# A hybrid encoder trunk on one core: one full tile traded for a value tile and a half tile, and other load costs in the planner

## The chip, the core and the metric

The kernel runs on one core of a Trainium2 chip. The core has a matrix engine (TensorE, called PE here; PEld is its loading of weights, which overlaps the matmuls), a vector engine (DVE), a scalar engine (ACT), GpSimd (POOL) and a sync engine (SP), which here issues every DMA. Each engine works through its own queue in order. Operands lie in SBUF, matmul results in banks of PSUM, and the inputs, the outputs and some intermediate tensors in DRAM.

The metric is the device time of one execution in microseconds. A version is timed in several runs, and their median counts.

## The reference

Two sequences (prompt and sample, each of 1024 positions of width 1024, float32) go through the same trunk of two layers. Each layer computes one projection into twelve blocks of 256 columns, four mixers, a gate for each, an output projection and a residual:

```python
def mixer_layer(x, norm_g, w_in, w_out, ...):
    hdn = rmsnorm(x, norm_g)
    z = jnp.einsum('bsd,dp->bsp', hdn, w_in)
    (a_v, a_g, b_q, b_k, b_v, b_g, c_u, c_g, d_q, d_k, d_v, d_g) = jnp.split(z, N_BLOCKS, axis=-1)
    y_a = pool_mixer(a_v, pool_w, pool_scale) * jax.nn.silu(a_g)
    y_b = dilated_attention(rope(heads(b_q)), rope(heads(b_k)), heads(b_v)).reshape(bsz, s, GROUP_W)
    y_b = y_b * jax.nn.silu(b_g)
    y_c = s5_mixer(c_u, a_re, a_im, log_dt, b_re, b_im, c_re, c_im, ssm_d, glu_w, glu_b) * jax.nn.silu(c_g)
    y_d = neighbourhood_attention(heads(d_q), heads(d_k), heads(d_v), na_rpb).reshape(bsz, s, GROUP_W)
    y_d = y_d * jax.nn.silu(d_g)
    y = jnp.concatenate([y_a, y_b, y_c, y_d], axis=-1)
    return x + jnp.einsum('bsm,md->bsd', y, w_out)

def trunk(x):
    for l in range(DEPTH):                 # DEPTH = 2
        x = mixer_layer(x, norm_g[l], w_in[l], w_out[l], ...)
    return rmsnorm(x, final_g)
```

The mixers are pooling over windows of 2 to 16 positions, attention in three dilated windows with rotary embedding, a bidirectional diagonal state space model (S5) and attention in a two-dimensional neighbourhood of 8 by 16 positions of a 16 by 64 grid. The heads are 64 wide, four in each attention.

## The kernel before

**Four passes.** The layers run in the order prompt, sample in layer 0, and then prompt, sample in layer 1; I number these passes 0 to 3. The x of a pass stays in SBUF, column major, as a high and a low part (`xh`, `xl`, eight tiles of 128 by 1024 each), so that a float32 product is made of three matmuls: `vz<-xh,whi`, `vz<-xl,whi` and `vz<-xh,wlo`. The parts of the weights, `whi` and `wlo`, are made from a loaded tile `raw` by ACT and POOL and kept in DRAM for the sample. These projections are most of PE's work.

**Steps.** A pass is made of steps, each a *thread* of operations, listed in `STEPS`: `setup0`/`setup1` (tables of the S5 mixer for a layer: POOL makes products `E` of tables named `turns`, which go to DRAM as `Rd`), `na` (neighbourhood attention), `sq` (sum of squares of the sample's x, function `sum_squares`), `poolw0`/`poolw1` (function `pool_weights`: the matrix `w_av` times `pool_w`, matmuls `rb<-th,wavt`, which makes the weights `wav` of the pooling mixer), `dil` (dilated attention, which ends with `combine`), `ssm` and `sout` (S5, in quads of groups that load `UM`, `Cm`, `R` and `B` and work on `X` and `H` on DVE), `pool`, `x` (normalisation of the next x), and the out stages (`out6723`, `out`), which load the old x into a tile `p`, add, and store.

**Neighbourhood attention.** For each of four heads `h` and four column windows `w`, sixteen windows in a pass, the loop in `neighbourhood` loads four pieces of 64 KB of values from `vd` in DRAM into a tile `nv` (group `v`) and, for some windows, a bias; it then makes scores, a softmax and transposes, splits the result into a tile `D`, and multiplies with the values in `outer` (six matmuls `no<-D,nv`, the last readers of `nv`).

**The list schedule.** No instruction is issued where it is written. Every call goes to a `Recorder`, which keeps the operations with what they depend on (`record`). `order` then plans: it walks through time with a cost for each operation (`cost`), a latency between engines (`LAT`), and a model of DMA, and each time an engine is free, it takes the ready operation of lowest `prio` for which there are buffers. Whether there are is the answer of `room`, which reserves for every earlier thread the most that it will still want of a group. Then `emit` replays the operations in the planned order, so that all instructions bear one line in the trace, L467 (L469 after the change). The plan decides which instruction stands before which on each queue and which tile goes into which buffer; when they run is decided on the chip by semaphores.

**Buffers.** SBUF is divided into groups of tiles of one size, counted in `SIZES`: `A`, full tiles of 128 partitions by 4 KB; `z`, *half tiles* of 128 by 2 KB; `v`, value tiles `nv` of 128 by 2 KB; `p`, tiles of the old x; `raw`, `whi`, `wlo`, `D` and others. A trace names a buffer after the first tile that lay in it: the six half tiles appear as `wto`, `th`, `fold` and `zq`, whatever they hold, and PSUM banks as `vz`, `kt`, `ss`, `rb` and `no`. So the weights `pool_w` land in a tile called `th`, and a load of the sample's x for `sq` reads `wto<-in_x`.

Of the kernel before, what the change touches and what calls it, by code (L numbers as in the profile page):

```python
# [145 lines left out]
def overlap(a, b):  # L146
    return a[0] <= b[1] and b[0] <= a[1] and (a[2] is None or b[2] is None or a[2] & b[2])


class Op:  # L150
    __slots__ = ("eng", "method", "args", "kw", "reads", "writes", "idx", "prio", "thread", "cost", "deps", "outs", "n", "ready", "end", "tiles", "pos", "start", "s", "e", "ev")


class Thread:
# [22 lines left out]
class Recorder:  # L177
# [61 lines left out]

    def record(self, eng, method, args, kw):  # L240
        op = Op()
        reserve, after = kw.pop("reserve", ()), kw.pop("after", None)
        op.eng, op.method, op.args, op.kw = NAMES[eng], method, args, kw
        pos = [a for a in args if isinstance(a, View)]
        op.writes = [kw[k] for k in ("out", "accum_out") if k in kw]
        if "out" not in kw:
            op.writes.insert(0, pos.pop(0))
        op.reads = pos + [v for k, v in kw.items() if isinstance(v, View) and k not in ("out", "accum_out")]
        op.idx, op.thread = len(self.ops), self.thread
        op.prio = op.idx + self.cls + self.base  # L250
        op.cost = self.cost(op)
        op.tiles = []
        deps = {}
        for write, views in ((False, op.reads), (True, op.writes)):
            for v in views:
                t = v.tile
                if t.space == "IO":
                    continue
                if t not in op.tiles:
                    op.tiles.append(t)  # L260
                whole = t.space == "PSUM"
                r = (0, 127, None) if whole else v.region()
                keep = []
                for o, w, q in t.accesses:
                    hit = (w or write) and overlap(q, r)
                    if hit and o is not op:
                        raw = w and not write
                        deps[o] = deps.get(o, False) or raw or o.eng != op.eng

                    covered = hit and write and o is not op and (whole or (r[2] is not None and r[0] <= q[0] and q[1] <= r[1] and q[2] | r[2] == r[2]))  # L270
                    if not covered:
                        keep.append((o, w, q))
                keep.append((op, write, r))
                t.accesses = keep
        if after is None and not deps:
            after = self.thread.ops[-1] if self.thread.ops else self.gate
        if after:
            deps.setdefault(after, False)
        op.deps = deps
        for v in reserve:  # L280
            if v.tile not in op.tiles:
                op.tiles.append(v.tile)
        for t in op.tiles:
            if not t.users:
                t.thread = self.thread
            t.users.append(op)
            t.left += 1
        op.pos = len(op.thread.ops)
        op.thread.ops.append(op)
        self.ops.append(op)  # L290
        return op
# [18 lines left out]
    def order(self):  # L310
# [14 lines left out]
        dma = 0.0  # L325
        done, result, now = 0, [], 0.0
# [42 lines left out]
        while done < len(self.ops):  # L369
            progress = False  # L370
            for e in engines:
# [3 lines left out]
                while q and q[0][0] <= now:  # L375
                    _, _, op = heapq.heappop(q)
                    heapq.heappush(r, (op.prio, op.idx, op))
                aside, pick, full = [], None, {}
                while r:
                    x = heapq.heappop(r)  # L380
# [8 lines left out]
                op, progress = pick, True  # L389
# [11 lines left out]
                if e == "SP":  # L401
                    v = op.writes[0]
                    size = 4
                    for _, n in v.dims:
                        size *= n
                    dma = max(dma, now + 1100) + size / 360.0
                    op.end = dma + 900
                result.append(op)
                done += 1
                th = op.thread  # L410
# [15 lines left out]
                for o, raw in op.outs:  # L426
                    lat = LAT.get((e, o.eng), 130)
                    if o.eng != e and o.thread.patient:
                        lat += SLACK
                    when = op.end + lat if raw else now  # L430
                    o.ready = max(o.ready, when)
                    o.n -= 1
                    if o.n == 0:
                        heapq.heappush(later[o.eng], (max(o.ready, now), o.idx, o))
# [9 lines left out]
            now = min(times)  # L444
# [32 lines left out]
    return v.rearrange("p (c j) -> p c j", c=4)  # L477


SIZES = dict(A=21, raw=2, whi=3, wlo=3, z=6, p=3, D=2, rs=2, v=1)  # L480
LATE, SOON = 10**6, -(10**6)
XLEAD, YLEAD, OB, RES, XG, NAORD, DILORD, NAHOLD, DILHOLD, NALOOP = 2, 3, ('mm', 's'), 1, 'p', ((('v', 'q'), ('q',)), (('v', 'q'), ('q',))), (('q', 'v'), ('q',)), -1, 0, 0
VB, FOLD = ('mm', 'mm', 'mm', 's'), 'vector'
# [5 lines left out]
class Kernel:  # L489
    def __init__(self, rec, T, nseq, depth, dbg=None):  # L490
        self.nc, self.nseq, self.depth = rec, nseq, depth
        self.T = {n: rec.extern(n, ap) for n, ap in T.items()}
        self.dbg = None if dbg is None else rec.extern("dbg", dbg)
        for name, n in SIZES.items():
            rec.group(name, n)
# [677 lines left out]
    def pool_weights(self, l):  # L1173

        nc = self.nc
        for m in range(2):
            made = self.own([128, 8, 128], "wav", F32, "DRAM")
            wt, pw = self.slot([128, S], "wavt"), self.z("pool_w")[:, :128]
            nc.sync.dma_start(out=wt, in_=self.T["w_av"][l, m])
            nc.sync.dma_start(out=pw, in_=self.T["pool_w"][:, l, m])  # L1180
            for i in range(2):
                ps, t = self.bank("t", "wav"), self.z("wav")
                for k in range(4):
                    nc.tensor.matmul(ps[:, 128 * k : 128 * k + 128], wt[:, 512 * i + 128 * k : 512 * i + 128 * k + 128], pw, start=True, stop=True)
                nc.scalar.activation(t, ps, AF.Copy)
                nc.sync.dma_start(out=made[:, 4 * i : 4 * i + 4], in_=t.rearrange("p (k x) -> p k x", k=4))
            self.made["w_in", l, MT_AV + m] = made
# [463 lines left out]
    def layer_out(self, s, l, keys, last):  # L1651
# [54 lines left out]
                    nc.sync.dma_start(out=self.T["y"][s, k, h], in_=t)  # L1706

    STEPS = (
        ("setup0", "na", "sq", "poolw0", "dil", "ssm", "sout", "pool", "x", "out6723", "out"),
        ("na", "dil", "ssm", "sout", "pool", "x", "out6723", "setup1", "poolw1", "out"),  # L1710
        ("na", "dil", "ssm", "sout", "pool", "x", "out6723", "out"),
    )
# [167 lines left out]
```

## Time and profile before

| | before |
|---|---|
| median of three runs | 2101.19 us (2095.68, 2101.19, 2106.34) |
| the profiled execution's own time | 2101.9 us |
| span of its trace | 2100.1 us |
| mean granted clock of PE | 0.973 |
| instructions in the trace | 33288 |

The median is of unprofiled runs. The trace is of one further execution; its span runs from the first to the last instruction, and its own time also holds the 1.8 us around that. All rows below are of this execution.

### The profile page before, as it was taken

The numbers are of one execution on the slowest core, as the hardware profiler recorded it, in microseconds if no ns is written. First come the engines' busy times: TensorE is split into PE (matmuls) and PEld (weight loads), VectorE is DVE, ScalarE is ACT, GpSimd is POOL, SyncE is SP. The second block draws the span as 40 slices with busy tenths as digits, with TensorE's granted clock in tenths as the row PEclk, the third lists the DMA queues.
The fourth block names the chain that finished last, engine by engine and source line by source line (L and its number), as shares of the span: only waits on it lengthen the run. The fifth ranks groups of instructions, "written<-read, shape, count | busy, mean of one in ns | idle before, by whom it ended". The sixth has DMA issues, their size and how long they took to land.

```text
span 2100.1 us, 33288 instructions
## 1 busy us (share of the span) xinstructions
PE 1960.8 (93%) x10996; PEld 1642.7 (78%) x10996; DVE 1531.7 (73%) x3353; ACT 1124.0 (54%) x2510; POOL 514.7 (25%) x416
## 2 busy tenths in 40 slices
PE   8997996997999999999979999999999999999997
PEld 7875875875788788878768788887878878888877
DVE  6977874899734556778878878779984556578855
ACT  4666584722435667833333666872343567783325
POOL 3223226143240010011033228213324001001103
PEclk8996998998999999999999999999999999999998
DMA  5455643474765544556876556356588754456575
GB/s 171 160 174 164 206 128 106 137 227 155 268 219 180 163 134 141 167 167 198 276 240 208 156 188 190 113 171 202 194 284 278 267 171 151 137 149 189 170 255 164
DMA packets 325308, 389.24 MB, mean 185 GB/s; under 512 B 51216, under 2 KB 196624, under 8 KB 325136
## 3 DMA queue, kind: packets, MB, share of 16 engines
q1 hardware_dynamic: 325136, 387.12, 58.4%
q8 instruction: 87, 1.43, 0.3%
q14 instruction: 85, 0.70, 0.1%
HBM read 274.91 MB, written 114.20 MB: 185 GB/s over the span
## 4 chain that ended last, share of the span: by engine, by line
PE 47%; DMA 14%; DVE 9%; issue 3%; SPq 2%; ACT 2%; POOL 0%; DVEq 0%; ACTq 0%; POOLq 0%
PE vz L467 34%; PE kt L467 4%; DMA nv<-vd 4%; PE no L467 4%; DMA p<-x 3%; PE rb L467 3%; PE ss L467 3%; SPq L467 2%; DMA x<-p 1%; DVE p L467 1%; DMA raw<-in_w_out 1%; DVE X L467 1%; DVE H L467 1%; DVE arena L467 1%; DVE wto L467 1%
## 5 line engine op out<-in xcount | busy, mean ns | idle before, releaser
L467 PE MATMUL vz<-xh,whi 128*128 128x512 f32 x1316 | 525.2, 399 | 16.7 <-DVE wto L467 14.6
L467 PE MATMUL vz<-xh,wlo 128*128 128x512 f32 x1316 | 526.4, 400 | 1.0 <-POOL wlo L467 0.6
L467 PE MATMUL vz<-xl,whi 128*128 128x512 f32 x1316 | 525.4, 399 | 0.3 <-DVE xl L467 0.3
L467 POOL TENSOR_TENSOR wlo<-raw,whi 128x512 fp32r<-128x512 f32 x128 | 193.0, 1510 | 479.5 <-ACT whi L467 387.5
L467 PEld LDWEIGHTS vz<-xh,whi 128*128 128x128 f32 x1316 | 248.7, 189 | 59.1 <-DVE wto L467 15.0
L467 ACT ACTIVATE whi<-raw 128x512 fp32r<-128x512 f32 x248 | 155.8, 629 | 249.1 <-DMA raw<-in_w_out 80.3
L467 PEld LDWEIGHTS vz<-xh,wlo 128*128 128x128 f32 x1316 | 248.6, 189 | 43.1 <-issue 2.3
L467 PEld LDWEIGHTS vz<-xl,whi 128*128 128x128 f32 x1316 | 248.5, 189 | 41.6 <-issue 1.2
L467 PE MATMUL vz<-whi,xh 128*128 128x256 f32 x480 | 138.9, 292 | 12.0 <-ACT xh L467 8.6
L467 PE MATMUL vz<-whi,xl 128*128 128x256 f32 x480 | 139.9, 292 | 0.5 <-DVE xl L467 0.3
L467 PE MATMUL vz<-wlo,xh 128*128 128x256 f32 x480 | 138.9, 291 | 0.0
L467 ACT ACTIVATE p<-p,st 128x256 f32<-128x256 f32 x256 | 128.1, 503 | 13.3 <-DVE st L467 11.9
L467 PE MATMUL vz<-yh,whi 128*128 128x512 f32 x288 | 115.7, 402 | 14.8 <-DVE p L467 10.6
L467 PE MATMUL vz<-yh,wlo 128*128 128x512 f32 x288 | 113.4, 395 | 0.6 <-DMA wlo<-low 0.6
L467 PE MATMUL vz<-yl,whi 128*128 128x512 f32 x288 | 113.4, 394 | 0.0
L467 DVE TENSOR_TENSOR D<-rb,D 128x256 fp32r<-128x256 f32 (+2 forms) x212 | 91.9, 454 | 19.7 <-ACT D L467 18.1
L467 PEld LDWEIGHTS vz<-whi,xh 128*128 128x128 f32 x480 | 94.5, 198 | 14.4 <-ACT xh L467 8.6
L467 DVE TENSOR_TENSOR p<-vz,p 128x512 f32<-128x512 f32 x81 | 55.3, 687 | 58.1 <-DMA p<-x 36.5
L467 ACT ACTIVATE D<-rb 128x256 fp32r<-128x256 f32 (+2 forms) x212 | 80.5, 412 | 31.1 <-PE rb L467 28.8
L467 PEld LDWEIGHTS vz<-whi,xl 128*128 128x128 f32 x480 | 95.1, 198 | 1.8 <-DVE xl L467 1.4
L467 PEld LDWEIGHTS vz<-wlo,xh 128*128 128x128 f32 x480 | 95.1, 198 | 0.2 <-issue 0.2
L467 ACT ACTIVATE p<-p,nmx 128x384 f32<-128x384 f32 x128 | 78.4, 614 | 24.2 <-DVE nmx L467 21.9
(464 smaller groups left out, 4515.9 us busy)
## 6 DMA issues: line engine op xcount, KB each, us to landing
raw<-in_w_in SPq DMA_DIRECT2D x176, 256.0 KB
low<-wlo SPq DMA_DIRECT2D x128, 256.0 KB
wlo<-low SPq DMA_DIRECT2D x120, 256.0 KB
x<-p SPq DMA_DIRECT2D x112, 256.0 KB
p<-x SPq DMA_DIRECT2D x88, 256.0 KB
nbias<-in_na_bias SPq DMA_DIRECT2D x48, 384.0 KB
nv<-vd SPq DMA_DIRECT2D x256, 64.0 KB
raw<-in_w_out SPq DMA_DIRECT2D x128, 128.0 KB
```

The costliest lines, as they stand in the source:

```text
L467: getattr(engines[op.eng], op.method)(*[real(a) for a in op.args], **{k: real(v) for k, v in op.kw.items()})
```

## The change

Four things change.

- **Sizes.** One full tile (4 KB a partition) is given up for a seventh half tile and a second value tile (2 KB each).
- **The model of loads in the plan.** A DMA is planned at 300 instead of 360 bytes per ns, and its result is planned to be there 1500 instead of 900 ns after the last byte. Nothing of this is in the emitted program, only in its order.
- **A margin.** An operation may be recorded with a `margin`, which the plan adds to the latency between engines before that operation. The `wav` matmuls in `pool_weights` get 4000 ns; every other operation gets 0.
- **The place of `sq`.** In pass 0, `sq` moves from behind `na` to behind `ssm`, so that it comes after `poolw0`, `dil` and `ssm` in the priority of buffers and operations.

```diff
@@ record
-        reserve, after = kw.pop("reserve", ()), kw.pop("after", None)
+        reserve, after, op.margin = kw.pop("reserve", ()), kw.pop("after", None), kw.pop("margin", 0)
@@ order
-                    dma = max(dma, now + 1100) + size / 360.0
-                    op.end = dma + 900
+                    dma = max(dma, now + 1100) + size / 300.0
+                    op.end = dma + 1500
...
                     if o.eng != e and o.thread.patient:
                         lat += SLACK
+                    if o.eng != e:
+                        lat += o.margin
                     when = op.end + lat if raw else now
...
-SIZES = dict(A=21, raw=2, whi=3, wlo=3, z=6, p=3, D=2, rs=2, v=1)
+SIZES = dict(A=20, raw=2, whi=3, wlo=3, z=7, p=3, D=2, rs=2, v=2)
@@ pool_weights
-  nc.tensor.matmul(ps[:, ...], wt[:, ...], pw, start=True, stop=True)
+  nc.tensor.matmul(ps[:, ...], wt[:, ...], pw, start=True, stop=True, margin=4000)
@@ STEPS
-        ("setup0", "na", "sq", "poolw0", "dil", "ssm", "sout", "pool", "x", "out6723", "out"),
+        ("setup0", "na", "poolw0", "dil", "ssm", "sq", "sout", "pool", "x", "out6723", "out"),
```

Since each of these goes into the plan, the whole order differs. Three places of it follow.

On SP, at the end of the neighbourhood loop of pass 1, before the change: `nv` is the value tile, `vd` the values in DRAM, `nbias` a bias, and `raw` and `wlo` are weights of the projections.

```order
L467 DMA wlo_528<-low_1835 128x512
L467 DMA nv_1008<-vd_5889 128x1x128 x4
L467 DMA raw_512<-in_w_in 128x512
L467 DMA wlo_534<-low_2371 128x512
L467 DMA raw_510<-in_w_in 128x512
L467 DMA nv_1008<-vd_5889 128x1x128 x4
L467 DMA nbias_6828<-in_na_bias 128x2x384
L467 DMA nv_1008<-vd_5889 128x1x128 x4
L467 DMA wlo_649<-low_2383 128x512
L467 DMA nv_1008<-vd_5889 128x1x128 x4
```

The same place after the change:

```order
L469 DMA nv_1018<-vd_5891 128x1x128 x4
L469 DMA nbias_6615<-in_na_bias 128x2x384
L469 DMA raw_510<-in_w_in 128x512
L469 DMA wlo_536<-low_1744 128x512
L469 DMA raw_512<-in_w_in 128x512
L469 DMA nv_1260<-vd_5891 128x1x128 x4
L469 DMA nbias_6679<-in_na_bias 128x2x384
L469 DMA nv_1018<-vd_5891 128x1x128 x4
L469 DMA nbias_6719<-in_na_bias 128x2x384
L469 DMA nv_1260<-vd_5891 128x1x128 x4
L469 DMA cos_6759<-in_cos 128x1024
L469 DMA sin_6766<-in_sin 128x1024
```

Before, all value loads go into one buffer, `nv_1008`; after, they go in turn into `nv_1018` and `nv_1260`, and loads of weights that stood between them stand ahead of them.

On POOL, in the dilated stage of pass 0, before the change: `E` and `turns` belong to `setup0`, `wlo` is the low part of a weight, `sin` is rotary work of the dilated mixer, and `wto` and `th` are half tiles.

```order
L467 TENSOR_TENSOR E_3755<-E_3755,wto_1796 128x512
L467 TENSOR_TENSOR wto_1796<-turns_2777 128x512
L467 TENSOR_TENSOR E_3755<-E_3755,wto_1796 128x512
L467 TENSOR_TENSOR wto_1796<-turns_2777 128x512
L467 TENSOR_TENSOR E_3808<-turns_2777 128x512 x2
L467 TENSOR_TENSOR E_3808<-E_3808,wto_1796 128x512
L467 TENSOR_TENSOR wto_1796<-turns_2777 128x512
L467 TENSOR_TENSOR E_3808<-E_3808,wto_1796 128x512
L467 TENSOR_TENSOR wlo_534<-raw_510,whi_526 128x512
L467 TENSOR_TENSOR th_1605<-th_1605,sin_1806 128x512
```

The rotary products of the dilated stage and those for `E`, after the change, where `zq`, `zr` and `fold` are half tiles:

```order
L469 TENSOR_TENSOR zq_1032<-turns_2712 128x512
L469 TENSOR_TENSOR E_3114<-turns_2712 128x512
L469 TENSOR_TENSOR E_3114<-E_3114,zq_1032 128x512
L469 TENSOR_TENSOR fold_1707<-fold_1707,sin_1858 128x512
L469 TENSOR_TENSOR zq_1032<-turns_2712 128x512
L469 TENSOR_TENSOR zr_1997<-turns_2712 128x512
L469 TENSOR_TENSOR E_3114<-E_3114,zq_1032 128x512
L469 TENSOR_TENSOR E_3246<-turns_2712 128x512 x2
L469 TENSOR_TENSOR E_3246<-E_3246,zr_1997 128x512
L469 TENSOR_TENSOR zr_1997<-turns_2712 128x512
L469 TENSOR_TENSOR fold_1873<-fold_1873,sin_1858 128x512
L469 TENSOR_TENSOR E_3246<-E_3246,zr_1997 128x512
```

Before, the last `sin` product comes when all products for `E` have been made; after, two `sin` products stand among those for `E`, the rest of which follow them.

On SP, loads of the sample's x for `sq` (`<-in_x`), before the change, in the neighbourhood loop of pass 0, with value loads and biases around them:

```order
L467 DMA nv_1008<-vd_960 128x1x128 x4
L467 DMA nbias_2098<-in_na_bias 128x2x384
L467 DMA wto_1876<-in_x 128x512
L467 DMA Kd_2118<-th_1777 128x112
L467 DMA nbias_2130<-in_na_bias 128x2x384
L467 DMA fold_1390<-in_x 128x512
L467 DMA th_1777<-in_x 128x512
L467 DMA th_1605<-in_x 128x512
L467 DMA nv_1008<-vd_960 128x1x128 x4
L467 DMA wav_2193<-wto_1876 128x512
```

After the change they stand in the SSM stage of pass 0, among loads of its tables (`UM`, `Cm`, `B`) and of weights:

```order
L469 DMA fold_1707<-in_x 128x512
L469 DMA fold_1381<-in_x 128x512
L469 DMA UM_4344<-Md_2797 128x512
L469 DMA Cm_4511<-Cd_2000 128x4x256
L469 DMA low_4515<-wlo_528 128x512
L469 DMA raw_512<-wav_2274 128x512
L469 DMA raw_510<-wav_2274 128x512
L469 DMA UM_4548<-ud_3831 128x512
L469 DMA zr_1997<-in_x 128x512
L469 DMA fold_1707<-in_x 128x512
L469 DMA B_4565<-Bd_1800 128x2x512
```

Every such load needs a free half tile when SP comes to it, and SP's queue stands until there is one; the loads have moved from the queue of the neighbourhood loop to that of the quads.

## Rows read from the trace of the kernel before

**Rows 1.** The page: busy us, share of the span and instructions; clock in 40 slices.

```profile
PE 1960.8 (93%) x10996; PEld 1642.7 (78%) x10996; DVE 1531.7 (73%) x3353; ACT 1124.0 (54%) x2510; POOL 514.7 (25%) x416
...
PEclk8996998998999999999999999999999999999998
```

**Rows 2.** Windows, the four passes: the first line names the columns.

```profile
core 0: us, PE busy (x) PEld busy (x) DVE busy (x) ACT busy (x) POOL busy (x), PEclk, DMA share, GB/s
0.00:616.00 616.00, 536.54 (x2903) 441.95 (x2904) 475.79 (x1033) 320.71 (x665) 218.91 (x170) 0.93 0.57 178
616.00:1116.00 500.00, 476.67 (x2666) 402.07 (x2666) 344.75 (x822) 266.50 (x611) 60.37 (x55) 0.99 0.58 182
1116.00:1614.00 498.00, 482.01 (x2757) 403.17 (x2757) 395.04 (x791) 268.93 (x614) 183.78 (x139) 1.00 0.63 198
1614.00:2100.00 486.00, 465.57 (x2676) 395.51 (x2675) 316.10 (x709) 267.87 (x621) 51.59 (x55) 0.99 0.58 184
```

**Rows 3.** Waits of PE: us in total, times, longest us.

```profile
PE vz L467 <- DVE wto L467: 17.9, 2, 14.6
PE no L467 <- DMA nv<-vd: 14.9, 24, 1.7
...
PE rb L467 <- DMA th<-in_pool_w: 7.8, 1, 7.8
PE ss L467 <- DMA UM<-Md: 5.3, 4, 2.4
```

**Rows 4.** The chain of waits around 700 us: start us, us, what.

```profile
698.81 4.46 DMA nv<-vd
```

**Rows 5.** The tile `nv` in pass 1: ns min/median/max, first and last start us.

```profile
L467 PE MATMUL no<-D,nv x96: 274/282/389, 662.5 to 763.5; 128*128 128x256 f32 x96
```

**Rows 6.** Waits of PE from 664 to 764 us, columns as in rows 3.

```profile
PE no L467 <- DMA nv<-vd: 3.2, 5, 1.7
```

**Rows 7.** Windows around 350 us in pass 0, columns as in rows 2.

```profile
340.00:350.00 10.00, 7.33 (x33) 5.75 (x31) 0.00 (x0) 0.00 (x0) 6.84 (x7) 1.00 0.46 131
350.00:367.00 17.00, 5.10 (x12) 4.04 (x13) 6.93 (x16) 9.06 (x12) 6.98 (x6) 0.50 0.35 99
```

**Rows 8.** Timeline of DVE: start us, us, instruction [idle before <-releaser].

```profile
354.64 0.21 DVE L467 TENSOR_TENSOR wto<-th 32x64 f32<-32x64 f32 x1 [14.82 <-POOL E L467]
```

**Rows 9.** Timeline of POOL, columns as in rows 8.

```profile
348.81 2.09 POOL L467 TENSOR_TENSOR E<-turns 128x512 f32<-128x512 f32 x2 [2.92 <-DMA Rd<-E]
```

**Rows 10.** A window in the neighbourhood loop of pass 0, columns as in rows 2.

```profile
152.00:201.00 49.00, 33.21 (x134) 22.80 (x133) 36.50 (x88) 32.91 (x79) 13.96 (x11) 0.58 0.54 154
```

**Rows 11.** Timeline of PE in that loop, columns as in rows 8.

```profile
155.70 0.35 PE L467 MATMUL no<-D,nv 128*128 128x256 f32 x1 [1.11 <-DMA nv<-vd]
...
200.78 0.36 PE L467 MATMUL no<-D,nv 128*128 128x256 f32 x1
...
210.10 0.28 PE L467 MATMUL no<-D,nv 128*128 128x256 f32 x1
```

**Rows 12.** Timeline of SP's queue in that loop: start us, us, DMA issue.

```profile
161.19 0.42 SPq L467 DMA_DIRECT2D nbias<-in_na_bias  x1
166.80 0.34 SPq L467 DMA_DIRECT2D wto<-in_x  x1
```

**Rows 13.** The chain of waits around 2000 us, columns as in rows 4.

```profile
2003.85 2.72 PE vz L467 x12
```

**Rows 14.** Timeline of PE in the out stage of pass 1, columns as in rows 8.

```profile
1063.12 2.05 PE L467 MATMUL rb<-th,wavt 128*128 128x128 f32 x8 [7.84 <-DMA th<-in_pool_w]
```

**Rows 15.** Groups by line and shape: busy us, mean ns of one | idle before, releasers.

```profile
L467 DVE TENSOR_TENSOR X<-X,R 128x512 f32<-128x512 f32 x32 | 36.3, 1141 | 3.0 <-POOL th L467 1.7 <-POOL wto L467 1.1
L467 DVE TENSOR_TENSOR X<-vz,R 128x512 f32<-128x512 f32 x16 | 10.9, 680 | 2.9 <-DMA R<-Rd 1.6 <-PE vz L467 0.6 <-PE kt L467 0.6
...
L467 POOL TENSOR_TENSOR ss<-ss,wto 128x512 f32<-128x512 f32 x19 | 24.8, 1310 | 122.2 <-ACT wto L467 120.3 <-DMA raw<-in_w_in 1.7
```

**Rows 16.** Windows in the SSM stage of pass 0, columns as in rows 2.

```profile
440.00:480.00 40.00, 34.28 (x208) 27.23 (x206) 36.65 (x42) 8.15 (x12) 20.83 (x16) 1.00 0.71 211
480.00:520.00 40.00, 30.12 (x129) 23.02 (x130) 37.84 (x50) 10.46 (x13) 11.62 (x5) 0.83 0.45 154
```

More of the change, by code (lines that the diff above doesn't have):

```diff
@@ L150 @@
 class Op:
-    __slots__ = ("eng", "method", "args", "kw", "reads", "writes", "idx", "prio", "thread", "cost", "deps", "outs", "n", "ready", "end", "tiles", "pos", "start", "s", "e", "ev")
+    __slots__ = ("eng", "method", "args", "kw", "reads", "writes", "idx", "prio", "thread", "cost", "deps", "outs", "n", "ready", "end", "tiles", "pos", "margin", "start", "s", "e", "ev")
 class Thread:
@@ L1183, in pool_weights @@
                 for k in range(4):
-                    nc.tensor.matmul(ps[:, 128 * k : 128 * k + 128], wt[:, 512 * i + 128 * k : 512 * i + 128 * k + 128], pw, start=True, stop=True)
+                    nc.tensor.matmul(ps[:, 128 * k : 128 * k + 128], wt[:, 512 * i + 128 * k : 512 * i + 128 * k + 128], pw, start=True, stop=True, margin=4000)
                 nc.scalar.activation(t, ps, AF.Copy)
```

## The prediction

> **What bounds the kernel now.** I read the page's busy rows first, then one row for each of the four passes (layer 0 prompt, layer 0 sample, layer 1 prompt, layer 1 sample), then the waits of PE, and last the stretches where PE stood. PE is busy 1960.8 of 2100.1 us; its granted clock is low in the slices at 160 to 210 us, 350 us and 490 us, where it had run out of work before [rows 1]. The first pass takes 616 us at a mean clock of 0.93, the other three 500, 498 and 486 us at 0.99 to 1.00 [rows 2]. So the kernel is bound by PE in passes 1 to 3, and what can still be won lies in pass 0 (about 110 us longer than the rest) and in single waits. PE's named waits are short: 17.9 us in two waits for a DVE copy out of PSUM, 14.9 us in 24 waits for a load of neighbourhood values (`nv<-vd`), 7.8 us in one wait for `pool_w`, 5.3 us for `UM<-Md` [rows 3].
>
> **The change, part by part.**
>
> *Two buffers for values.* With one tile `v`, the four loads of a window can only be issued when the previous window's `outer` has read the tile. The chain shows it: a load of 4.46 us stands in it in one window [rows 4], and the like in others. The sixteen windows of pass 1 take 101 us (662.5 to 763.5), 6.3 us each [rows 5]. With two tiles the loads of the next window are issued during this one, as the order shows on SP, so the load leaves the chain. What it is worth is what PE waits, not what the chain shows, since projections fill PE meanwhile: 3.2 us in pass 1's loop [rows 6], so some 10 of the 14.9 us in passes 1 to 3, and the rest in pass 0 (counted below with it). I take **-9 us**; the bounds are 0 (DVE or ACT ends the same waits a little later) and -15 (all of it).
>
> *Half tiles and POOL's order in pass 0.* From 340 to 350 us DVE does nothing at all, and to 367 us PE works 12.4 of 27 us, 5.1 of them at half clock [rows 7]; here lies the longest of PE's waits, 14.6 us at a matmul whose PSUM bank DVE has not emptied [rows 3]. DVE in turn stands 14.82 us for POOL's `E<-E,wto` [rows 8]: its next result (of the dilated `combine`) goes into the half tile `wto`, which POOL still reads for the last products of `setup0`, and POOL has itself just waited 2.92 us for a store of `E` to land [rows 9]. So the half tiles are out, and the one to come free depends on a slow chain. The change adds a seventh, and in its order POOL's products for `E` come earlier: the last `sin` product of the dilated stage stood behind all of `E`; now two of them stand among the products for `E`, and the others follow. The stall should go. PE's work in the 27 us is 7.3 us and 5.1 at half clock, some 10 us at the full one, so 17 us is the most that is directly saved. I take **-15 us**. Bounds: 0, if the half tiles run out at the earlier place of `E` instead, and -22, where the clock before and behind it gains too.
>
> *Neighbourhood loop of pass 0.* From 152 to 201 us PE is busy 33.2 of 49 us at a clock of 0.58 [rows 10]. In the order of before no projection stands between the `outer`s of five windows there; they begin at 155.70 and end at 200.78 us, 9.0 us each, and the next `outer`, with 22 projection matmuls ahead of it, begins at 210.10 [rows 11]. SP, too, stands from 161.61 to 166.80 us at a load of `sq` (the sum of squares of the sample), which needs a free half tile [rows 12]. The change takes `sq` out of this place and gives a seventh half tile. But it also has one full tile less, and in its order six windows, to the end of the loop, stand without a projection; the 22 matmuls come after it (5.0 us, estimated from twelve in 2.72 us, a row of the chain [rows 13]). At 7.0 us a window, between 6.3 [rows 5] and 9.0, six windows are 42, against 54.4 now: 42 + 5.0 - 54.4 = **-7 us**. Bounds: -12 at 6.3 and +5 at 9.0.
>
> *pool_w and its margin.* In the out stage of pass 1 PE stands 7.84 us at a `wav` matmul, the head of its queue, until `pool_w` has landed [rows 14]; that load had waited for a half tile that an earlier `wav` store was still reading. With seven half tiles, and 4 us more in the plan before a `wav` matmul is placed, it goes. The out stage has waits of its own for loads of the old x, which can take part of it back: **-5 us**, between 0 and -9.
>
> *The model of loads* (1500 instead of 900 ns, 300 instead of 360 bytes per ns) costs nothing by itself; it puts consumers of loads later in each queue. Its cover is other projection work on PE, which is there except in pass 0's loop. Together with the missing full tile it is my one loss: **+4 us**, between 0 and 15 (one more stall as long as the longest that PE has now, 14.6 us [rows 3]).
>
> *The place of sq.* Sixteen loads, sixteen squares on ACT and fourteen adds on POOL move from the loop to the SSM stage of pass 0. ACT is idle over 70% there; POOL's adds take 1310 ns each [rows 15], 18 us in a stretch of 80 us in which POOL is busy 32 [rows 16]. Its result is needed only for the sample's x, well after. I cost it at 0; the cover is POOL's idle time, and if that is not where the adds stand, the case is the second rival.
>
> Sum: -9 - 15 - 7 - 5 + 4 = -32 us on 2100.1 us, so 2068 us; with the 1.8 us by which the profiled run's own time (2101.9) exceeds its span, 2070. The median of the runs shown is 2101.2, 0.7 below the profiled run, so **2069 us**.
>
> **A rule against the change.** DVE's `X<-X,R` (both inputs in SBUF) takes 1141 ns on average, `X<-vz,R` of the same shape with one input in PSUM 680 ns [rows 15]; the former often runs beside a POOL product. The Trainium skill, page "SBUF — State Buffer", section "Who interferes with whom", says that a DVE instruction with two SBUF inputs and a GpSimd instruction that reads SBUF lock each other out for a whole instruction. The rows agree. By that rule, if all fourteen adds of `sq` met such DVE work in a stage where DVE is busy 37 of 40 us, they would add an estimated 14 x 1.31 = 18 us, and the sum would be 2087; by my reading they already met DVE work at their old place, and it stays 2069.
>
> **Rivals.**
> 1. *The gains of pass 0 do not reach the end.* Behind the hole at 350 us DVE is busy 36.7 and 37.8 of 40 us [rows 16], and what PE wins before, it waits there. Then only the values and `pool_w` count: 2101 - 14 + 4 = 2091. For it speaks DVE's load; against it that DVE itself stood idle through the hole, so that its work moves up as well.
> 2. *Slower.* In the SSM stage the order on SP puts loads of `sq` before the `UM` and `Cm` loads of the quads. One such load held SP for 5.2 us at its old place [rows 12]. Eight such holds, two to each of the four quads, are 42 us in a stage where DVE has no slack; with the -32 that is +10, 2111. It decides from about 8 us a quad on; PE's waits for `UM` are 5.3 us in all now [rows 3], and there are seven half tiles, both against it.
> 3. *More than the sum.* The loops run at the pace of ACT and DVE, the clock in pass 0 stays up, and each gain comes to its far bound: -15 - 22 - 12 - 9 + 4 = -54, some 2047.
>
> **How the numbers follow.** Forecast (2054 to 2088): 0.48. Rival 1 (2085 to 2105): 0.24. Rival 2 (above 2105): 0.12. Rival 3 (below 2054): 0.16. The runs shown spread by 0.5% (2095.7 to 2106.3), so 10.5 us is about what can be told from no change. Faster by more than that (below 2090.7): the forecast, rival 3 and nearly a third of rival 1, 0.71. Slower (above 2111.7): most of rival 2, 0.09. The rest, 0.20, is the same. The range that holds 8 in 10 runs from 2034, at the far end of rival 3 (its gains and a little more in pass 0's clock), to 2102, inside rival 1.
>
> **What would show it.** Right: PE's waits for `nv<-vd` fall from 14.9 to under 4 us; no DVE idle of more than 5 us between 300 and 400 us; no PE wait for `pool_w` over 2 us; the first pass ends near 594 instead of 616 us while the others come out 3 to 8 us shorter. Wrong: waits of PE for `UM<-Md` or `H` above 15 us in pass 0, a low clock in slices that are full now, or passes 1 to 3 longer by more than 5 us each, which would mean that the missing full tile costs more than the second value tile gives.

## The result and the profile after

The changed kernel takes 2070.59 us (median; 2068.99 to 2072.21), 30.3 us less than the kernel before beside it (2100.91 us); the ratio is 0.9847 (95% interval 0.982 to 0.9874). The forecast was 2069 us, in a range of 2034 to 2102.

The page of the changed kernel, to be read against [rows 1], shows where 29.7 us of span went: PE is busy 10.2 us less (its clock is 0.977 instead of 0.973 on average) and idle 19.5 us less, 119.8 instead of 139.3.

```profile
PE 1950.6 (94%) x10996; PEld 1646.2 (80%) x10996; DVE 1538.4 (74%) x3353; ACT 1122.9 (54%) x2510; POOL 502.3 (24%) x416
...
PEclk9996999999999999999999999999999999999999
```

The low clock at 350 and 490 us has gone; the one in the neighbourhood loop of pass 0 (fourth slice) has stayed. The four passes, columns as in [rows 2], the first and the third, divided as there where the last matmul of a pass's out stage ends (a small one, `rb<-ones,ss` or `rb<-ones,rstd`, that sums squares for the next normalisation):

```profile
0.00:598.00 598.00, 532.94 (x2937) 446.11 (x2937) 484.13 (x1034) 322.64 (x665) 216.63 (x171) 0.95 0.59 185
...
1088.00:1595.00 507.00, 487.61 (x2771) 409.52 (x2769) 388.21 (x780) 267.72 (x614) 172.74 (x141) 0.99 0.62 195
```

Against [rows 2] the passes are 18 shorter, 10 shorter, 9 longer and 11 shorter. This division does not leave the same work on its two sides (2903 matmuls in pass 0 before, 2937 after). The last matmul of the output projection itself does, within one matmul; in pass 0 it is a `kt<-yh,wlo` that ends at 604.6 us before and at 584.1 after. The windows up to it and behind it, first before, then after:

```profile
0.00:604.60 604.60, 526.54 (x2822) 432.28 (x2822) 474.41 (x1031) 318.07 (x660) 214.09 (x165) 0.93 0.56 177
604.60:2100.10 1495.50, 1434.24 (x8176) 1210.42 (x8174) 1057.28 (x2322) 805.94 (x1850) 300.56 (x251) 0.99 0.60 189
...
0.00:584.10 584.10, 519.22 (x2823) 432.59 (x2824) 481.93 (x1030) 318.87 (x659) 209.74 (x165) 0.94 0.58 183
584.10:2070.40 1486.30, 1431.40 (x8175) 1213.62 (x8173) 1056.44 (x2323) 804.03 (x1851) 292.53 (x252) 0.99 0.60 190
```

Divided there, pass 0 is 20.5 us shorter and the rest 9.2: pass 1 is 3.9 shorter (495.1 for 499.0), pass 2 is 1.4 longer (499.5 for 498.1), and the last, to the end of the span, 6.6 shorter (491.8 for 498.4).

The waits of PE, to be read against [rows 3]:

```profile
PE vz L469 <- ACT xh L469: 12.9, 3, 8.6
PE rb L469 <- ACT fold L469: 10.4, 3, 5.3
...
PE no L469 <- DMA nv<-vd: 4.0, 6, 1.0
```

The two waits for `wto` (17.9 us), that for `pool_w` (7.8) and those for `UM` (5.3) are gone, and loads of values cost 4.0 us instead of 14.9. I added up all rows of this view by the engine that ended the wait, for this kernel and for those of the experiments:

| us | all | by a DMA | by DVE | by ACT |
|---|---|---|---|---|
| before | 131.1 | 34.3 | 76.7 | 17.2 |
| changed | 112.1 | 4.0 | 64.8 | 38.6 |

So 30 us of waits for DMAs are gone, and with them the 14.6 us for DVE in pass 0; 21 us have come as new waits for ACT.

The tile `nv` in pass 1, against [rows 5]: the sixteen windows take 85.4 us (640.8 to 726.2) instead of 101.

```profile
L469 PE MATMUL no<-D,nv x96: 274/282/384, 640.8 to 726.2; 128*128 128x256 f32 x96
```

The longest wait of DVE for POOL, which was 14.82 us [rows 8], is 2.4 us:

```profile
DVE X L469 <- POOL wto L469: 2.4, 1, 2.4
```

At the `wav` matmuls of pass 1's out stage [rows 14] PE now waits 4.36 us, for ACT and no longer for a load; in pass 0 the same work stands in the neighbourhood loop, where PE waits 5.33 us. Timeline of PE at both places:

```profile
154.72 2.08 PE L469 MATMUL rb<-zq,wavt 128*128 128x128 f32 x8 [5.33 <-ACT fold L469]
...
1040.08 2.08 PE L469 MATMUL rb<-fold,wavt 128*128 128x128 f32 x8 [4.36 <-ACT fold L469]
```

Pass 2 is the one that did not become shorter. Its last output stage takes 72 us instead of 60 (windows, 1523 to 1595 and 1554 to 1614), at a clock of 0.95 instead of 1.00; PE waits 3.82 us there for `xh`, a wait that the kernel before does not have in this pass. Why that wait came was not followed further. Of the 12 us, 4 are only the small matmuls of the sums, which stand further behind the projection (16.5 us instead of 11.8); the other 8 are nearly made good by the part of the pass ahead of this stage.

### The profile page after: what moved, and what is told of

Its sections match the earlier page's. It is cut to its first block, busy times and chain, and to the rows that moved or that the text cites. A ratio compares the mean times of both kernels' runs of the same rounds, so it can differ in the third digit from the quotient of the medians.

```text
span 2070.4 us, 33332 instructions
## 1 busy us (share of the span) xinstructions
PE 1950.6 (94%) x10996; PEld 1646.2 (80%) x10996; DVE 1538.4 (74%) x3353; ACT 1122.9 (54%) x2510; POOL 502.3 (24%) x416
## 4 chain that ended last, share of the span: by engine, by line
PE 54%; DVE 8%; DMA 6%; ACT 2%; issue 2%; SPq 1%; POOL 0%; DVEq 0%; ACTq 0%; POOLq 0%
PE vz L469 39%; PE kt L469 6%; PE no L469 3%; PE rb L469 3%; PE ss L469 3%; DMA p<-x 2%; DVE arena L469 1%; DVE p L469 1%; DMA nv<-vd 1%; ACT fold L469 1%; DMA raw<-in_w_in 1%; SPq L469 1%; DVE X L469 1%; DVE gate L469 1%; ACT K L469 1%
## 5 line engine op out<-in xcount | busy, mean ns | idle before, releaser
L469 PE MATMUL vz<-whi,xh 128*128 128x256 f32 x448 | 129.1, 292 | 19.2 <-ACT xh L469 8.6
L469 PE MATMUL vz<-whi,xl 128*128 128x256 f32 x448 | 129.8, 291 | 0.6 <-DVE xl L469 0.6
L469 PE MATMUL vz<-wlo,xh 128*128 128x256 f32 x448 | 129.3, 291 | 0.0
L469 PE MATMUL vz<-yh,whi 128*128 128x512 f32 x252 | 100.7, 402 | 11.9 <-DVE p L469 8.0
L469 PEld LDWEIGHTS vz<-whi,xh 128*128 128x128 f32 x448 | 87.9, 198 | 21.7 <-ACT xh L469 8.6
L469 PE MATMUL vz<-yl,whi 128*128 128x512 f32 x252 | 99.9, 397 | 0.0
L469 PE MATMUL vz<-yh,wlo 128*128 128x512 f32 x252 | 99.1, 393 | 0.0
L469 PE MATMUL rb<-c_ident,p 128*128 128x128 f32 x504 | 90.1, 280 | 8.5 <-DVE D L469 7.8
L469 PE MATMUL no<-D,bv 128*128 128x256 f32 x512 | 91.0, 295 | 6.3 <-DVE fold L469 4.2
L469 DVE TENSOR_TENSOR p<-vz,p 128x512 f32<-128x512 f32 x73 | 49.8, 687 | 60.4 <-DMA p<-x 50.6
```

What stands on the lines that cost most here:

```text
L469: getattr(engines[op.eng], op.method)(*[real(a) for a in op.args], **{k: real(v) for k, v in op.kw.items()})
```

## The experiments

Theory 1 was that of the prediction: each part has its price, and the prices add. Theory 2 was that the whole order counts, and that any edit of the plan's numbers gives another order that is some 10 us better or worse by accident. Undoing single parts of the changed kernel and two placebos came first. How much an edit moves is the number of PE's 10348 planned operations that do not keep their order (those outside the longest common sequence of the two plans); the change itself moves 3081.

**One value tile again (a_v1).**

```diff
-SIZES = dict(A=20, raw=2, whi=3, wlo=3, z=7, p=3, D=2, rs=2, v=2)
+SIZES = dict(A=20, raw=2, whi=3, wlo=3, z=7, p=3, D=2, rs=2, v=1)
```

> The changed kernel with one value tile (v=1) again; seven half tiles, twenty full tiles, the new model of loads, the margin and the new place of sq stay. Theory 1 (each part is worth its own term, and the second value tile is worth 9 us): 2080 (2071 to 2086), PE's waits for nv<-vd back at 12 to 15 us, sixteen windows of a later pass back at about 100 us from 86. Theory 2 (the new order as a whole matters, single parts have no price of their own): anywhere within 15 us of 2071, on either side, with the windows slow again. Theory 3 (the second value tile is nearly all of the gain): 2093 or more.

2093.83 us (2083.96 to 2098.7), ratio to before 0.9955 (0.9933 to 0.9977): 23 us lost. Waits for `nv<-vd` are 8.5 us, and the windows of pass 1 take 107 us. It is above what theory 1 gave and reads like theory 3, but a later run (b_load) is as fast as the changed kernel with one value tile. The edit moves 3007 of PE's operations, about as many as the change itself, so that the 23 us cannot be put down to the buffer alone.

**Six half tiles again (a_z6)**, with `z=6` and `v=2` in the same line.

> The changed kernel with six half tiles again; two value tiles and all else stay (2 KB a partition lie unused). Theory 1 (the seventh half tile takes away DVE's hole in the dilated stage of pass 0 and the wait for pool_w): 2071 + 15 + some 4 = 2090 (2080 to 2098), with a hole of DVE of over 8 us between 280 and 380 us and a PE wait for pool_w of over 4 us in the out stage of pass 1. Theory 2 (order as a whole): within 15 us of 2071, hole or no hole. Theory 3 (the second value tile is nearly all): 2071 to 2075.

2087.07 us (2082.85 to 2089.75), ratio 0.9927 (0.9902 to 0.9952). The number is theory 1's, but neither of its signs is there: PE does not wait for `pool_w` at all, the hole of DVE does not come back, and 12 of the 16 us are lost in pass 2, where I had expected nothing. The edit moves 2131 of PE's operations. The longest waits of DVE for POOL in this kernel:

```profile
DVE fold L469 <- POOL fold L469: 2.8, 2, 2.5
```

**The old model of loads (a_load).**

```diff
-                    dma = max(dma, now + 1100) + size / 300.0
-                    op.end = dma + 1500
+                    dma = max(dma, now + 1100) + size / 360.0
+                    op.end = dma + 900
```

> The changed kernel with the old model of loads in the plan (360 bytes per ns, 900 ns). Theory 1 (my term: the new model costs some 4 us): 2067 (2056 to 2071). Rival (the new model is itself a gain, since its plan puts consumers of loads where the loads have landed): 2080 or more, with more and longer waits of PE for DMAs than the changed kernel has (nv<-vd 4.0 us there). Theory 2 (order as a whole): within 15 us of 2071 on either side, without a wait that answers to it.

2094.02 us (2086.37 to 2098.35), ratio 0.9964 (0.9946 to 0.9981): 23 us lost where I had forecast a gain of 4. But PE's waits ended by a DMA only rise from 4.0 to 8.1 us, so the rival's reason covers 4 of the 23. The edit moves 2985 of PE's operations.

**Two placebos (a_load3, a_l1550)**: 1495 and 1550 instead of 1500 ns in the same line, which move 297 and 1935 of PE's operations.

> A placebo: the changed kernel with 1495 instead of 1500 ns in the plan's model of loads. No size, margin or step differs, but the plan comes out in another order nearly everywhere after the first pass's start. Theory 1 (parts have their price, the order's accidents little): 2071 within 5 us. Theory 2 (order as a whole): 8 us or more away from 2071 on either side, as much as the runs that undo a part.

> A second placebo that moves far more than the first: the changed kernel with 1550 instead of 1500 ns in the plan's model of loads moves some 1900 of PE's 10348 operations and 400 of SP's 1937 out of their order (the first placebo moved 300 and 84; the old model of loads moves 3000 and 650). If the old model costs its 23 us because loads planned too early make engines wait, this one stays at 2071 within 6 us. If it cost them because any order other than this one is worse by accident, this one is 10 to 20 us slower too.

2071.65 us (2070.29 to 2074.84) and 2080.0 us (2077.99 to 2082.27). The small one changes nothing. The large one is 9.4 us slower than the changed kernel with no overlap of the runs, although PE's waits ended by a DMA are 3.6 us in it, as few as in the changed kernel; those for DVE are 81.4 instead of 64.8, those for ACT 24.6 instead of 38.6. An accident of the order is worth some 10 us here. In the traces it lies in pass 0: up to the last matmul of its output projection that pass takes 592.0 us instead of 584.1, and the rest takes 1486.2 and 1486.3.

**sq at its old place (a_sq), and no margin (a_margin0).**

```diff
-        ("setup0", "na", "poolw0", "dil", "ssm", "sq", "sout", "pool", "x", "out6723", "out"),
+        ("setup0", "na", "sq", "poolw0", "dil", "ssm", "sout", "pool", "x", "out6723", "out"),
```

```diff
-... start=True, stop=True, margin=4000)
+... start=True, stop=True, margin=0)
```

> The changed kernel with sq back behind na in pass 0; sizes, margin and model of loads stay. Theory 1 (my terms: sq itself costs nothing at either place, but taking it out of the neighbourhood loop is part of the 7 us there): 2074 (2071 to 2081), with SP standing at a load of the sample's x for over 3 us in the loop of pass 0, and the first pass ending later by about that much. Theory 2 (order as a whole): some 700 of PE's 10348 operations change their place, within 8 us of 2071 on either side.

> The changed kernel with the margin of the wav matmuls at 0. Theory 1 (my term of 5 us for pool_w is the margin's and the seventh half tile's together): 2073 to 2076, with a PE wait for pool_w of 3 us or more. Rival (with seven half tiles pool_w is there in time anyway): 2071 within 4 us and no such wait. Theory 2 (order as a whole): some 1400 of PE's operations change their place, 8 us or more away from 2071 on either side.

2071.64 us (2068.5 to 2071.95) and 2068.11 us (2064.36 to 2071.24): neither differs from the changed kernel beyond its runs, though they move 699 and 1438 of PE's operations. Without the margin no wait for `pool_w` appears.

**The new sizes alone, on the kernel before (b_sizes)**: the line of `SIZES` only.

> The kernel before with the new sizes alone (20 full tiles, seven half tiles, two value tiles). Theory 1 (terms add: values 9, half tiles 15, part of the loop and of pool_w): 2075 (2068 to 2083). Theory of pairs (buffers and the new model of loads need each other, as three runs that each undo one part and lose 16 to 23 us make likely): 2085 to 2098, which is what undoing the model of loads gave.

2074.22 us (2072.24 to 2080.64), ratio 0.9872 (0.9843 to 0.9901): 27 of the 30 us. It differs from a_load only in the margin and the place of sq, and is 20 us faster; in the traces the difference lies almost wholly in pass 0 (583 against 603 us, see the table below). Here, with seven half tiles, no margin and the old model, the wait for `pool_w` is there (timeline of PE):

```profile
1024.13 2.04 PE L467 MATMUL ss<-fold,wavt 128*128 128x128 f32 x8 [6.10 <-DMA fold<-in_pool_w]
```

**The new model of loads alone, on the kernel before (b_load)**: 300 and 1500 in the two lines, old sizes.

> The kernel before with the new model of loads alone (300 bytes per ns, 1500 ns), old sizes. My term: 2105 (2101 to 2116). If the new model is a gain of its own, as undoing it in the changed kernel (23 us slower, 2 to 9 us in each pass) suggests: 2080 to 2092. If it needs the buffers, since loads planned to take longer hold their tiles for longer: 2098 to 2110.

2071.35 us (2067.04 to 2072.88), ratio 0.9853 (0.9831 to 0.9875): as much as the whole change, with one value tile, six half tiles and 21 full ones. But the gain lies in pass 0: up to the last matmul of its output projection that pass takes 577.6 us, 27.0 less than before, and the rest is 2.0 shorter, although 16 of the 22 us of waits for DMAs that went were in the rest (9.5 us there, before 25.3).

```profile
577.60:2071.10 1493.50, 1434.18 (x8175) 1215.44 (x8174) 1050.66 (x2324) 805.48 (x1852) 299.09 (x252) 0.99 0.60 189
```

PE does not wait for `pool_w`, and for values (waits of PE) it waits

```profile
PE no L467 <- DMA nv<-vd: 10.5, 13, 2.4
```

**One full tile less and nothing for it (b_A20), and then the same order with two value buffers (c_v2).** The second deals the value tiles out in turn after the plan is made, so that no instruction changes its place:

```diff
+    def reslot(self, result, group, n):
+        left, free, slot = {}, list(range(n)), {}
+        for op in result:
+            for t in op.tiles:
+                if t.group == group:
+                    left[t] = left.get(t, 0) + 1
+        for op in result:
+            for t in op.tiles:
+                if t.group == group:
+                    if t not in slot:
+                        slot[t] = free.pop(0)
+                    left[t] -= 1
+                    if left[t] == 0:
+                        free.append(slot[t])
...
-    rec.emit(tc, rec.order())
+    result = rec.order()
+    rec.reslot(result, "v", 2)
+    rec.emit(tc, result)
```

> The kernel before with 20 full tiles instead of 21, and nothing given for it (4 KB a partition lie unused): the price of the missing full tile, and the base of the next run. My term put it inside 4 us: 2101 to 2110. If the full tile bought nothing: 2101 within 4 us; if every new order differs by accident as the second placebo did: up to 10 us on either side.

> The same order as the run with 20 full tiles, instruction by instruction on every engine; after the plan is made, the value tiles are dealt to two buffers in turn instead of one. Only waits can go, no work moves. If the second value tile is worth the waits for loads that PE shows (my reading): 5 to 10 us less than that run, PE's waits for nv<-vd from about 15 to under 6 us. If its worth is what the planner makes of it (loads issued a window ahead, windows closer together): within 4 us of that run, since in that order the loads of a window still stand behind work that waits for the window before it.

b_A20 takes 2089.92 us (2082.02 to 2092.19), ratio 0.9937 (0.9912 to 0.9962). Fewer buffers cannot speed anything up by themselves; this kernel is faster than the one before because its order is another, which moves 2395 of PE's operations. DVE's hole is absent here too, with six half tiles (waits of DVE for POOL, the longest):

```profile
DVE fold L467 <- POOL th L467: 1.4, 1, 1.4
```

c_v2 takes 2083.03 us (2079.56 to 2085.21), ratio 0.991 (0.9889 to 0.9932): 6.9 us less than b_A20; the two intervals overlap at their ends. The waits of PE for values, first of b_A20 and then of c_v2:

```profile
PE no L467 <- DMA nv<-vd: 20.3, 24, 1.9
```

```profile
PE no L485 <- DMA nv<-vd: 15.2, 17, 2.0
```

So the time is inside the first of the two ranges expected, but the waits are not: a second buffer in an unchanged order takes 5 of the 20 us of them, and the windows of pass 1 hardly come closer (98.7 us, from 102). The rest of the waits goes where the plan knows of the buffer: in b_sizes, with the old model of loads, 0.7 us of them are left.

**The two combined otherwise (mix)**: the kernel before with the new sizes, and the new model of loads for passes 1 to 3 only.

```diff
+                    first = op.thread.name.endswith("_0") or op.thread.idx < 3
+                    dma = max(dma, now + 1100) + size / (360.0 if first else 300.0)
+                    op.end = dma + (900 if first else 1500)
```

> The kernel before with the new sizes, and the new model of loads only for threads of passes 1 to 3; sq at its old place, no margin. The new sizes alone end their first pass at 583 us against 598 in the changed kernel, which in turn is 2 to 9 us shorter in each later pass. If these add: 2056 to 2066. If the order of the later passes is an accident of where the first one ends: 2066 to 2082.

2060.27 us (2057.81 to 2064.55), ratio 0.9806 (0.9782 to 0.9829): the fastest of all, 41 us below before and some 10 below the changed kernel, whose runs it does not overlap. Both halves came as the first of the two expectations has it: up to the last matmul of pass 0's output projection it takes 570.4 us (b_sizes 572.7), and from there 1485.6 (the changed kernel 1486.3). The windows behind that matmul, first of b_sizes, then of mix, which differs from it by the model of loads in passes 1 to 3 alone (columns as in [rows 2]):

```profile
572.70:2070.50 1497.80, 1434.05 (x8176) 1214.40 (x8174) 1056.15 (x2323) 803.07 (x1851) 297.99 (x251) 0.99 0.59 188
...
570.40:2056.00 1485.60, 1433.57 (x8164) 1214.27 (x8163) 1054.78 (x2324) 805.35 (x1851) 304.24 (x252) 0.99 0.60 190
```

All runs in one table: the time, PE's waits by what ended them, the length of each pass in the trace (between the last matmuls of two out stages; the last one to its own last matmul, some 6 us before the span ends), and the two parts of the span up to and behind the last matmul of pass 0's output projection.

| run | us | waits by a DMA | by DVE and ACT | passes 0, 1, 2, 3 | pass 0, rest |
|---|---|---|---|---|---|
| before | 2100.9 | 34.3 | 93.9 | 616, 500, 498, 480 | 604.6, 1495.5 |
| changed | 2070.6 | 4.0 | 103.4 | 598, 490, 508, 469 | 584.1, 1486.3 |
| a_v1 | 2093.8 | 11.8 | 101.6 | 600, 502, 505, 477 | 589.1, 1502.0 |
| a_z6 | 2087.1 | 3.4 | 109.0 | 600, 491, 520, 467 | 586.9, 1497.5 |
| a_load | 2094.0 | 8.1 | 118.2 | 603, 496, 510, 478 | 593.2, 1500.3 |
| a_load3 | 2071.7 | 3.6 | 98.4 | 602, 488, 507, 466 | 586.7, 1482.9 |
| a_l1550 | 2080.0 | 3.6 | 106.0 | 604, 490, 504, 474 | 592.0, 1486.2 |
| a_sq | 2071.6 | 4.0 | 101.9 | 601, 490, 504, 469 | 585.9, 1484.2 |
| a_margin0 | 2068.1 | 5.2 | 98.3 | 597, 490, 508, 467 | 584.1, 1485.4 |
| b_sizes | 2074.2 | 14.5 | 93.4 | 583, 492, 511, 478 | 572.7, 1497.8 |
| b_load | 2071.4 | 12.3 | 92.0 | 593, 489, 506, 476 | 577.6, 1493.5 |
| b_A20 | 2089.9 | 32.9 | 89.5 | 596, 496, 509, 481 | 583.0, 1505.1 |
| c_v2 | 2083.0 | 30.3 | 83.9 | 596, 493, 510, 475 | 581.4, 1499.2 |
| mix | 2060.3 | 5.2 | 90.6 | 585, 492, 508, 463 | 570.4, 1485.6 |

Three things run through it. The waits ended by a DMA follow the edits and not accident: 30 to 34 us with old model and old order of the value loads, 12 to 15 with either the sizes or the model, 3 to 5 with both (8 in a_load, which has the old model, and 12 in a_v1, which has one value tile). And the first pass is 12 to 33 us shorter than before in every other order, whatever the buffers. And the last column separates the runs: behind pass 0's output projection the six kernels with both the new sizes and the new model there (changed, the two placebos, a_sq, a_margin0, mix) take 1483 to 1486 us, the eight that lack some of it 1494 to 1505, the kernel before 1496. Neither part alone shortens this stretch (b_sizes 2 longer, b_load 2 shorter), all together take 9 to 13 us off it. These are single executions, and the division is not quite even: 2822 to 2835 matmuls stand ahead of that place, and 13 of them, which start some 0.23 us apart in a projection, are an estimated 3 us. Up to that place there is no such grouping: 570 to 593 us, against 605 before.

## Why the prediction was right, and which of its steps were not

The forecast held in its total, 2069 against 2070.6 us, in the first pass (598 us, forecast near 594), and in its signs but one: waits for values fell to 4.0 us (forecast: under 4, so at the edge), no idle time of DVE over 5 us is left between 300 and 400 us, PE no longer waits for `pool_w`, and waits for `UM<-Md`, the sign of the second rival, are gone. That passes 1 to 3 each come out 3 to 8 us shorter did not hold: they are 10 shorter, 9 longer and 11 shorter, or, divided at the output projections, 3.9 shorter, 1.4 longer and 6.6 shorter. That the total is within 2 us is luck in part: a placebo moves pass 0 by 8 us, and two of the terms failed in their reason or their sign. By its terms:

- **Two value tiles, -9 us.** Right in size as a wait: 14.9 us of waits fell to 4.0. That the second buffer alone does it was not shown: c_v2, which adds nothing else to b_A20, loses a quarter of these waits and gains 6.9 us, with intervals that overlap. In the changed kernel the plan also uses the buffer to set the windows closer together (85 instead of 101 us), and undoing it there costs 23; what of the 23 is the buffer's and what the other order's was not told apart.
- **Half tiles and POOL's order in pass 0, -15 us.** The hole went, as forecast, but the step that gave this to the seventh half tile failed. In a_z6, b_A20 and b_load, with six half tiles, DVE's wait of 14.82 us is absent as well. It belonged to the order of before, and none of the other orders tried here has it.
- **The neighbourhood loop of pass 0, -7 us.** Small, as forecast: the sixteen windows take 130 instead of 134 us in the trace. Six windows without a projection go at 6.4 us each (166.0 to 204.5 us), better than the 7.0 that I took, but `wav` matmuls now stand ahead of them, with the wait of 5.33 us shown above.
- **`pool_w`, -5 us.** The wait for the load went, and 4.36 us of wait for ACT took its place at the same work. The half tile was the wrong reason (b_sizes has seven and still waits 6.10 us). The margin or the new model of loads is enough: the wait is there in the four kernels that have neither (before, b_sizes, b_A20, c_v2), and PE does not wait for `pool_w` in a_load, which has the margin and the old model, nor in a_margin0, b_load and mix, which have the new model in that pass and no margin.
- **The model of loads, +4 us.** The step that failed: I costed it as a loss because it moves the consumers of loads back in their queues, and left out what it takes away. With the new sizes it is worth 12 to 14 us in passes 1 to 3 (b_sizes to mix, 1497.8 to 1485.6; a_load to the changed kernel, 1500.3 to 1486.3). In the first of these pairs PE's waits ended by a DMA in passes 1 to 3 fall with it, from 12.7 to 2.7 us; in the second only from 5.8 to 4.0, so that these waits are not the whole reason. Alone it takes PE's waits ended by a DMA from 34.3 to 12.3 us, and passes 1 to 3 become 2 us shorter; the other 27 us are pass 0's.
- **The place of `sq`, 0.** Right: a_sq is 1.0 us from the changed kernel. The eight `X<-X,R` of DVE in the SSM stage of pass 0 take 1321 ns each beside the adds of `sq` and 1217 ns in a_sq without them (groups by line, 335 to 480 us, first the changed kernel, then a_sq), together 0.8 us. The fourteen adds of `sq` take 22.9 us there, 1.64 us each; in a_sq, in the neighbourhood loop, they take 21.3 (1.52 each).

```profile
L469 DVE TENSOR_TENSOR X<-X,R 128x512 f32<-128x512 f32 x8 | 10.6, 1321 | 0.7 <-POOL fold L469 0.5 <-POOL zr L469 0.2
```

```profile
L469 DVE TENSOR_TENSOR X<-X,R 128x512 f32<-128x512 f32 x8 | 9.7, 1217 | 2.1 <-POOL kt L469 2.1
```

  A single one of them takes 0.66 us when it begins ahead of POOL's instruction (417.00 us) and 1.78 when it begins behind (398.65 us); it then ends at 400.43 us, 0.55 after POOL's instruction (399.88). Timelines of POOL and DVE in the changed kernel:

```profile
398.14 1.74 POOL L469 TENSOR_TENSOR wlo<-raw,whi 128x512 fp32r<-128x512 f32 x1
398.65 1.78 DVE L469 TENSOR_TENSOR X<-X,R 128x512 f32<-128x512 f32 x1
```

  The rule of the Trainium skill, page "SBUF — State Buffer", section "Who interferes with whom", bears on these rows: one side stands for the other's whole instruction when they meet, and the trace agrees. But the 18 us that I had worked out from it did not reach the end: only two of the eight `X<-X,R` begin behind an add of `sq` (at 445.24 and 469.10 us), and the others that wait do so behind work that POOL has there anyway.

So the sum came out right with one term of the wrong sign, and with terms that do not add: the sizes alone give 27 us, the model alone 30, both with margin and new place of `sq` 30, both in mix 41. They do not take away the same waits: the sizes alone leave 0.7 us of the waits for values and all of that for `pool_w`, the model alone leaves 10.5 us for values and nothing for `pool_w`. What they share is pass 0, where each alone is 32 and 27 us shorter than before, the changed kernel 20.5 and mix 34; behind it neither gains without the other. The order's accidents come on top: 9 us between two models of loads that differ by 50 ns.

What is left open: how much of the 20.5 us of pass 0, and of the 27 of b_load there, is owed to a part and how much to the leaving of an unlucky order, since a placebo on the kernel before was not run. That each of the twelve other orders, the changed kernel's among them, is faster than the one before (by 6 to 41 us), one of them with less memory and nothing else changed, speaks for a good part of the latter; the hole in pass 0 and the low clock behind it are its visible piece, and they lie in the first pass, which is 12 us or more shorter everywhere. Nor is it settled why a_load loses 20 us to b_sizes in pass 0, or why passes 1 to 3 need both parts: PE's waits ended by a DMA do not explain it alone, since a_z6 and a_load have 3.4 and 5.8 us of them there, the changed kernel 4.0, and they take 11 and 14 us longer.

## What to carry to other kernels

Where a planner sets the order, first divide the span at an instruction that has the same work ahead of it in both orders, and compare stage by stage: by their totals b_sizes and b_load each look like the whole change, and both won their time in pass 0 alone. Then run a placebo before crediting a part: an edit of a constant that should not matter, large enough to move as much of the order as the part does. Read single parts from the waits that they should remove, and not from the total alone, and hold the order fixed (deal the buffers out again after planning) where the question is what a buffer is worth. Try the plan's model of loads together with the buffers and not only one by one: it takes no memory, and in passes 1 to 3 neither was worth anything here without the other.

## What the runs showed of the hardware that was not expected

POOL's `E<-turns`, which reads one tile of SBUF, is 1076 ns at its fastest in the changed kernel and 2056 ns at its slowest, in one stretch of 40 us (the tile `E`, minimum, median and maximum). The slowest begins at 274.83 us, beside DVE's `wto<-fold,cos` of 1.08 us at 274.92, and is longer by about as much. A wait on such a chain cannot be planned with one number.

```profile
L469 POOL TENSOR_TENSOR E<-turns x8: 1076/1084/2056, 264.9 to 302.7; 128x512 f32<-128x512 f32 x8
```
